# A hybrid decoder layer on one Trainium2 core: the hand-written order at the start of the FFN, carried on to the end of pair 1

## The chip, the cores and the metric

The kernel runs on one core of a Trainium2 chip. TensorE multiplies matrices, VectorE and GpSimd do elementwise work, ScalarE does copies, casts and activation functions, and SyncE issues most of the DMAs. The metric is the device time of one execution in microseconds, median of several runs; lower is better. The profile names the engines PE, DVE, POOL, ACT and SP, in this order.

## The reference

One layer for a prompt of 512 tokens and a sample group of 64 tokens, 576 in all, width 1024. The stage that matters here is the output projection of the mixer with its norms, and the first half of the feed-forward network (FFN):

```python
x = x + rms_norm(jnp.einsum('btd,de->bte', merged, w_out), norm_post_mix)
h = rms_norm(x, norm_pre_ffn)
gate, up = jnp.split(jnp.einsum('btd,df->btf', h, w_ffn_in), 2, axis=-1)
x = x + rms_norm(jnp.einsum('btf,fd->btd', jax.nn.silu(gate) * up, w_ffn_out), norm_post_ffn)
```

`gate` and `up` are 2816 wide each, 22 tiles of 128 columns.

## The kernel before

**Numbers in two parts.** Each fp32 operand is split into a high part (a cast on ScalarE) and a low part (operand minus high, on VectorE), and a product is three matmuls: high by high, high by low, low by high. `split` (activations) and `wsplit` (weights) emit the cast and the subtraction.

**Pairs.** The FFN's first half goes in 22 pairs; pair m is gate tile m and up tile m. For each pair the program does seven products (Strassen's scheme in Winograd's form over the two halves of the contraction and of the tokens) instead of eight. A product is four contraction tiles by three terms, twelve matmuls of 288 columns (`prod`). Steps 0 and 1, the "leads", take the plain activations B1 and the gate weights as loaded. Steps 2 to 6 take sums of activation quadrants (TQ[0] to TQ[3] and B2) and sums of weight quadrants, each split into two parts after it was made. Steps 2, 4 and 6 add up in PSUM bank p, steps 3 and 5 in bank e; after steps 2 and 3 ScalarE copies the bank (`as_`, `eu`), after steps 4, 5 and 6 VectorE reads it.

**Activation sums.** Token tiles 1 to 4 hold 128 prompt tokens, tile 0 the sample tokens. When a tile has its two norms, TensorE transposes it (`turn`). For tiles 1, 2 and 0 `left` splits it and copies it to `hf`; the tiles 3, 4 and the right part of tile 0 are then summed with it by class `Sums` (s3, s4, s0): `two` makes t[0] = b12 - b11 and t[1] = b22 - t[0] on VectorE, `late` makes t[1] - b11 and b21 - t[1] in place on GpSimd, and `split(i)` splits sum i. TQ[1] (step 2) holds t[1], TQ[0] (step 3) t[0], TQ[2] (step 4) the new b11, B2 (step 5) b22, TQ[3] (step 6) the new b21.

**Weight sums.** `pair_sums` makes the four sums in place in the raw gate and up tiles (`wraw` or `ad`, and `wup`), one of them always on GpSimd, all of them there for pair 0 (`slow`). Tiles are reused in rings: two `wraw`, two `wup`, two of each split pair (`w2`, `w22`, `w`), seven scratch tiles `ev`, five PSUM tiles `bank` and three `mmps`. A load into a reused tile waits until its last reader is done: pair 4's gate tile is loaded into pair 0's, pair 5's into pair 1's.

**What sets the order.** A scheduler orders the instructions of each engine by its own planning. Between `order.__enter__()` and `order.__exit__()` the instructions of TensorE, ScalarE, VectorE and GpSimd stand as written; the scheduler may still put later ones in between. Before, this written part covers the norms of the five tiles, the leads of pairs 0 to 3 and all splits of the activation sums; what follows (`run`, steps 2 to 6 of pair 0 and all other pairs) is left to the scheduler. SP's loads are always placed by it.

Of the kernel before, what the change touches and what calls it, by code (L numbers as in the profile page):

```python
# [93 lines left out]
def _build(ctx, tc, I, O):  # L94
# [1059 lines left out]
    class Sums:  # L1154
# [3 lines left out]
        def two(self):  # L1158
            b11, b12, b21, b22 = self.b
            self.t = [ev(KH * self.n).rearrange("p (a b) -> p a b", b=self.n) for _ in range(2)]  # L1160
            tt(self.t[0], b12, b11, ALU.subtract)
            tt(self.t[1], b22, self.t[0], ALU.subtract)

        def late(self):
            b11, b12, b21, b22 = self.b
            G.tensor_tensor(out=b11, in0=self.t[1], in1=b11, op=ALU.subtract)
            G.tensor_tensor(out=b21, in0=b21, in1=self.t[1], op=ALU.subtract)
# [14 lines left out]
    class Tile_:  # L1182
# [79 lines left out]
    def pair_sums(rg, ru, slow=False):  # L1262
        def sub(out, a, b, op=ALU.subtract, g=slow):
            (G if g else V).tensor_tensor(out=out, in0=a, in1=b, op=op)  # L1264

        a22 = two(fw, "w22", [P, KH, P], 2)
        S.copy(out=a22[0], in_=ru[:, KH:])
        sub(a22[1], ru[:, KH:], a22[0])
        sub(ru[:, KH:], ru[:, :KH], ru[:, KH:], ALU.add)
        sub(ru[:, :KH], rg[:, :KH], ru[:, :KH], g=True)  # L1270
        sub(rg[:, :KH], ru[:, KH:], rg[:, :KH])
        sub(rg[:, KH:], rg[:, KH:], rg[:, :KH])
        return a22

    def half_split(raw):
        g = two(fw, "w2", [P, KT, P], 2)
# [87 lines left out]
    prs = {}  # L1364
# [14 lines left out]
    act(warm, warm, AF.Silu)  # L1379
# [18 lines left out]
    ps = tile_mm(0)  # L1398
    wo_half(0, 0, ps)
# [10 lines left out]
    firsts = [pair_first(rg[0])]  # L1410
# [8 lines left out]
    firsts.append(pair_first(rg[1]))  # L1419
# [15 lines left out]
    av = [fp.tile([P, T], F32, name=f"av{k}") if not 4 <= k < 16 else None for k in range(FT)]  # L1435
    fwc = ExitStack()
    fw = fwc.enter_context(pool("fw", 1, reuse_waits="tile"))
    for m in range(4):
        raw = rg[m] if m < 2 else raw_load(dbl[m - 2][:, :KT * P].rearrange("p (k m) -> p k m", m=P), m * P)
        prs[m] = Pair(m, raw)  # L1440
        if m < 2:
            prs[m].w = firsts[m]
    ru = raw_up(0)
# [4 lines left out]
    prs[0].lead()  # L1448
    T_[3].turn(mmt)
    t4.resid()  # L1450
    prs[1].lead()
    prs[0].lead_out()
    t4.stat2()
    prs[2].first()
    s3 = Sums(*T_[3].pv, slice(C_OF[3], C_OF[3] + P), P)
    s3.two()
# [171 lines left out]
```

## Time and profile before

| | us |
|---|---|
| median of three runs | 1244.08 |
| lowest and highest of them | 1239.37, 1244.59 |
| the profiled execution | 1235.15 |
| its span, first to last instruction | 1233.4 |
| TensorE, VectorE, ScalarE, GpSimd busy | 1143.2, 720.1, 571.5, 150.0 |
| first matmul of pair 0's lead | 805.77 |
| first matmul of pair 0's step 2 | 835.52 |
| first matmul of pair 2's step 2 | 860.91 |

The last three are moments in the profiled execution, counted from the span's start. The idle time in brackets behind a row is that of the row's engine just ahead of it, and the name behind the arrow is what ended it. "L125" and the like are lines of helpers, so products are told apart by their tiles: `w` with `b1h` is a lead, `w22` or `w2` with `mh` or `b2h` one of the steps 2 to 6, `ident` a transpose.

### The profile page before, as it was taken

To read this page: it belongs to the slowest core of one execution; us is meant where nothing else is said; L and a number is where in the kernel's file an instruction comes from. 1 tells how busy PE (TensorE), PEld (TensorE's weight loads), DVE (VectorE), ACT (ScalarE), POOL (GpSimd) and SP (SyncE) were. 2 spreads that over 40 slices of the span, in tenths; PEclk is the share of its full clock that TensorE was granted. 3 is DMA by queue.
4 is the path that set the end of the run, shared out by engine and by line. 5 is a ranking of instruction groups with operands and counts; after the bars stand their busy time and mean duration, and the time that the engine had idled before them with its cause. 6 is when DMAs were issued, how large, how long until landed. Compare 5 with 4: busy or idle time off the path is not lost.

```text
span 1233.4 us, 20309 instructions
## 1 busy us (share of the span) xinstructions
PE 1143.2 (93%) x8104; PEld 1070.4 (87%) x8104; DVE 720.1 (58%) x1385; ACT 571.5 (46%) x1226; POOL 150.0 (12%) x227
## 2 busy tenths in 40 slices
PE   5699999999998998799998997978999999999997
PEld 4699999998997988698988895868999999978885
DVE  5136742566884456687554654677777888661323
ACT  4232532785554673377454533435454454441221
POOL 3200121001000011010000100141111110160001
PEclk9899999999997999899999999988999999999999
DMA  7730344333534353635133754022323332312222
GB/s 187 186 80 1 95 121 129 78 75 107 117 91 104 82 108 86 181 83 152 53 107 76 257 174 137 1 69 69 97 77 101 103 104 87 102 52 86 84 87 77
DMA packets 162001, 125.24 MB, mean 102 GB/s; under 512 B 13856, under 2 KB 144449, under 8 KB 161907
## 3 DMA queue, kind: packets, MB, share of 16 engines
q1 hardware_dynamic: 154770, 102.15, 31.4%
q0 software_dynamic: 6848, 21.22, 5.1%
q8 instruction: 63, 1.03, 0.3%
q10 hardware_dynamic: 288, 0.59, 0.2%
q14 instruction: 32, 0.25, 0.1%
HBM read 106.87 MB, written 17.06 MB: 100 GB/s over the span
## 4 chain that ended last, share of the span: by engine, by line
PE 43%; DMA 9%; issue 7%; DVE 5%; ACT 4%; POOL 1%; POOLq 0%; DVEq 0%; ACTq 0%; SPq 0%
PE mmps L267 11%; PE bank L1286 8%; PE bank L1561 6%; PE mmps L1561 6%; PE mmps L1286 5%; DMA wraw<-w_ffn_in 2%; PE bank L1179 2%; DMA out_sd_s<-Si 1%; PE mmps L1179 1%; DMA Si<-state_delta 1%; ACT whi L251 1%; DMA ev<-gcd 1%; DMA wraw<-w_out 1%; DVE wlo L125 1%; DVE w2lo L125 1%
## 5 line engine op out<-in xcount | busy, mean ns | idle before, releaser
L267 PE MATMUL mmps<-xh,whi 128*128 128x256 f32 (+1 forms) x896 | 274.2, 306 | 3.7 <-ACT ev L137 3.2
L267 PE MATMUL mmps<-xh,wlo 128*128 128x256 f32 (+1 forms) x896 | 271.4, 304 | 1.6 <-DVE wlo L125 1.6
L267 PE MATMUL mmps<-xl,whi 128*128 128x256 f32 (+1 forms) x896 | 272.5, 304 | 0.0
L125 DVE TENSOR_TENSOR wlo<-wraw,whi 128x1024 fp32r<-128x1024 f32 x114 | 147.4, 1293 | 211.5 <-ACT whi L251 211.3
L251 ACT CAST whi<-wraw 128x1024 fp32r<-128x1024 f32 x114 | 119.4, 1049 | 228.6 <-PE mmps L267 81.9
L267 PEld LDWEIGHTS mmps<-xh,whi 128*128 128x128 f32 x896 | 174.9, 195 | 6.7 <-ACT ev L137 4.2
L267 PEld LDWEIGHTS mmps<-xh,wlo 128*128 128x128 f32 x896 | 175.0, 196 | 2.3 <-DVE wlo L125 1.9
L267 PEld LDWEIGHTS mmps<-xl,whi 128*128 128x128 f32 x896 | 175.2, 196 | 0.4 <-issue 0.2
L128 DVE SCALAR_TENSOR_TENSOR ev<-ev,fcol 128x600 f32<-128x600 f32 x72 | 60.1, 837 | 1.8 <-ACT ev L137 0.6
L137 ACT ACT_TABLE_LOAD x41 | 52.6, 1283 | 6.9 <-DVE ans L125 2.6
L1286 PE MATMUL bank<-mh,w2hi 128*128 128x288 f32 x156 | 48.0, 308 | 4.8 <-ACT w2hi L251 4.7
L1286 PE MATMUL bank<-mh,w2lo 128*128 128x288 f32 x156 | 47.5, 305 | 2.3 <-DVE w2lo L125 2.3
L1286 PE MATMUL bank<-ml,w2hi 128*128 128x288 f32 x156 | 47.3, 303 | 0.0
L1264 POOL TENSOR_TENSOR wup<-wraw,wup 128x512 f32<-128x512 f32 x20 | 26.1, 1307 | 173.4 <-DVE wup L1264 173.3
L137 ACT ACTIVATE ev<-mmps 128x320 f32<-128x320 f32 (+1 forms) x73 | 30.7, 430 | 31.1 <-PE mmps L267 19.5
L137 ACT ACTIVATE jk<-bank 128x128 bf16<-128x128 f32 (+1 forms) x112 | 31.2, 279 | 25.3 <-PE bank L933 19.3
L378 PE MATMUL bank<-vh,xh 128*128 128x346 f32 (+1 forms) x96 | 31.1, 330 | 9.7 <-ACT vh L251 9.7
L267 PE MATMUL mmps<-oal,whi 128*128 128x320 f32 (+1 forms) x128 | 37.6, 296 | 1.0 <-DVE oal L125 1.0
L267 PE MATMUL mmps<-obl,whi 128*128 128x320 f32 (+1 forms) x128 | 37.9, 298 | 0.0
L267 PE MATMUL mmps<-oah,wlo 128*128 128x320 f32 (+1 forms) x128 | 37.5, 296 | 0.2 <-DVE wlo L125 0.2
L267 PE MATMUL mmps<-obh,wlo 128*128 128x320 f32 (+1 forms) x128 | 37.5, 296 | 0.0
L267 PE MATMUL mmps<-oah,whi 128*128 128x320 f32 (+1 forms) x128 | 37.2, 298 | 0.3 <-ACT oah L295 0.2
(500 smaller groups left out, 2989.0 us busy)
## 6 DMA issues: line engine op xcount, KB each, us to landing
wraw<-w_in SPq DMA_DIRECT2D x56, 512.0 KB, 8.6
wup<-w_ffn_in SPq DMA_DIRECT2D x22, 512.0 KB, 4.7
wraw<-w_ffn_out SPq DMA_DIRECT2D x22, 512.0 KB, 3.8
wraw<-w_ffn_in SPq DMA_DIRECT2D x20, 512.0 KB, 3.9
pgd<-ev POOLq DMA_DIRECT2D x16, 288.0 KB, 4.2
ev<-pgd SPq DMA_DIRECT2D x16, 288.0 KB, 8.3
wraw<-w_proj_b SPq DMA_DIRECT2D x8, 512.0 KB, 3.9
Si<-state_delta SPq DMA_DIRECT2D x8, 512.0 KB, 8.0
```

The lines of the kernel that those rows point to most:

```text
L125: V.tensor_tensor(out=out, in0=a, in1=b, op=op)
L128: V.scalar_tensor_tensor(out=out, in0=a, scalar=s, in1=b, op0=op0, op1=op1)
L137: return S.activation(out=out, in_=a, func=f, scale=scale, accum_out=accum)
L251: S.copy(out=hi, in_=raw)
L267: TE.matmul(ps, lhsT=a[:, j, :], rhs=b[k][:, HF[hf]], start=(k == 0 and i == 0), stop=(k == nk - 1 and i == 2))
L378: TE.matmul(ps, lhsT=a[k] if t == 0 else a[k][:, o:o + P], rhs=b[:, k, :c1 - c0], start=(k == 0 and q == 0), stop=(k == KT - 1 and q == le ...
L1179: TE.matmul(ps[q], lhsT=a[k] if t == 0 else a[k][:, o:o + P], rhs=b[k][:, q * 512:(q + 1) * 512], start=(k == 0 and i == 0), stop=(k == KT ...
L1264: (G if g else V).tensor_tensor(out=out, in0=a, in1=b, op=op)
L1286: TE.matmul(ps, lhsT=w[x][:, j], rhs=b[y][:, j], start=(first and j == 0 and i == 0), stop=(j == KH - 1 and i == 2), skip_group_check=not ...
L1561: TE.matmul(ps, lhsT=x[k] if t == 0 else x[k][:, o:o + P], rhs=unit[w][:, a_], start=(k == 0 and i == 0), stop=(k == FT - 1 and i == len(t ...
```

## The change

The written order goes on: it now also holds steps 2 to 6 of pairs 0 and 1 and the weight preparation of pairs 1 and 2, and the scheduler's part begins with `run(2)`. Within it:

- The chain of tile 4's second norm (`resid`, `stat2`, `scale`) comes ahead of the sums and of the Silu of the leads; `lead_out` is parted into the addition (`lead_add`) and the Silu (`lead_act`), and the Silus stand behind step 2 and later.
- The activation sums are made one at a time by `Sums.one(i)`, all on VectorE, each just ahead of its split and of the step that needs it; `two` and `late` are gone.
- The weight sums are all on VectorE; the first goes to a scratch tile `ev` (`s1`) instead of into `wup`, and the order of the quadrants is arranged anew, so that steps 3 and 6 take other split tiles (`w22` is now step 3, `w2` step 6; pair 0's step 2 has a `w22` tile of its own).
- Pair 0's bank e is an `mmps` tile, tile 4's transposes go to one `bank` and one `mmps`, and ScalarE's copy of pair 2's first bank stands ahead of the split of tile 3's b22 (`s3.split(4)`).
- `Pair.rest`, used for all later pairs, follows the new arrangement: one temporary more, nothing on GpSimd.

- The Silu on the one-column tile `warm` is written a few lines later; ScalarE's order around it is the same.

The matmuls are the same in number and shape. The diff, cut:

```diff
-        def two(self):
+        def one(self, i):
             b11, b12, b21, b22 = self.b
-            tt(self.t[0], b12, b11, ALU.subtract)
-            tt(self.t[1], b22, self.t[0], ALU.subtract)
-        def late(self):
-            G.tensor_tensor(out=b11, in0=self.t[1], in1=b11, op=ALU.subtract)
-            G.tensor_tensor(out=b21, in0=b21, in1=self.t[1], op=ALU.subtract)
...
+            out, x, y = ((self.t[0], b12, b11), (self.t[1], b22, self.t[0]), (b11, self.t[1], b11), (b21, b21, self.t[1]))[i]
+            tt(out, x, y, ALU.subtract)
...
-    def pair_sums(rg, ru, slow=False):
...
+        def sums(self):
+            ru, rg = raw_up(self.m) if self.m else ru0, self.rg
+            self.s1 = ev(KH * P).rearrange("p (k m) -> p k m", m=P)
+            tt(self.s1, ru[:, :KH], ru[:, KH:], ALU.add)
+            tt(ru[:, :KH], rg[:, :KH], ru[:, :KH], ALU.subtract)
+            tt(rg[:, :KH], self.s1, rg[:, :KH], ALU.subtract)
+            self.ru = ru
+        def sum4(self):
+            tt(self.rg[:, KH:], self.rg[:, KH:], self.rg[:, :KH], ALU.subtract)
...
     t4.scale()
-    a22 = pair_sums(rg[0], ru, True)
-    prs[1].lead_out()
-    s3.split(4)
...
+    p2_.p, p3_.p = bank()[:, :TH], bank()[:, :TH]
+    p2_.q = mmt()[:, :TH]
+    prod(p2_.p, p2_.w[0], BQ[0], True)
+    S.copy(out=p2_.g[:, L_], in_=p2_.p)
+    t4.turn(iter((bank, mmt)))
+    prod(p2_.q, p2_.w[1], BQ[1], True)
...
+    s3.split(4)
+    p1_.lead_add()
+    p3_.first()
+    s4.one(0)
+    s4.one(1)
...
+    p0_.sums()
+    p0_.w[2] = split_of("w22", p0_.rg[:, :KH], KH)
+    p0_.lead_act()
+    p1_.lead_act()
+    p0_.step(2)
+    p3_.lead_add()
     for x in (s0, s3, s4):
         x.split(0)
+    p0_.split1()
+    p0_.step(3)
+    p2_.lead_act()
+    p3_.lead_act()
+    for x in (s0, s3, s4):
+        x.one(2)
+        x.split(2)
+    p0_.split3()
+    p0_.step(4)
+    s0.split(4)
+    s4.split(4)
+    p0_.sum4()
+    p0_.w[5] = [g[:, KH:] for g in split_of("w2", p0_.rg, KT)]
+    p0_.step(5)
+    for x in (s0, s3, s4):
+        x.one(3)
+        x.split(3)
+    p1_.sums()
+    p1_.sum4()
+    p0_.step(6)
...
-    for m in range(FT):
+    for m in range(2, FT):
         run(m)
```

ScalarE between pair 0's steps 3 and 4. Before, the casts of the sums (`hf`) stand one behind the other, and the bank copies (`COPY ev`) come after them:

```order
L251 CAST w2hi<-wup 128x1024
L295 CAST mh<-hf 128x4x128
L295 CAST mh<-hf 128x4x32
L295 CAST mh<-hf 128x4x128
L295 CAST b2h<-hf 128x4x32
L295 CAST b2h<-mmps 128x4x128
L295 CAST mh<-hf 128x4x128
L295 CAST mh<-hf 128x4x32
L295 CAST mh<-hf 128x4x128
L251 CAST whi<-wraw 128x1024
L1346 COPY ev<-bank 128x288
L1351 COPY ev<-bank 128x288
```

Now, with step 3's copy (`COPY ev<-mmps`) first and pair 4's gate cast (`whi<-wraw`) behind step 5's weights:

```order
L1371 COPY ev<-mmps 128x288
L137 ACTIVATE av_8422<-av_8422 128x288
L137 ACTIVATE av_8423<-av_8423 128x288
L295 CAST mh<-hf 128x4x32
L295 CAST mh<-hf 128x4x128 x2
L251 CAST w2hi<-wup 128x1024
L295 CAST b2h<-hf 128x4x32
L295 CAST b2h<-mmps 128x4x128
L251 CAST w2hi<-wraw 128x1024
L1301 CAST whi<-wraw 128x1024
```

The copy and the two Silus moved ahead of the casts, and the up weights' cast (`w2hi<-wup`) behind them.

VectorE at the same place. Before, the low parts (`ml`, `b2l`) stand without sums between them:

```order
L125 TENSOR_TENSOR w2lo<-wup,w2hi 128x1024
L125 TENSOR_TENSOR ml<-hf,mh 128x4x128
L125 TENSOR_TENSOR ml<-hf,mh 128x4x32
L125 TENSOR_TENSOR ml<-hf,mh 128x4x128
L125 TENSOR_TENSOR b2l<-hf,b2h 128x4x32
L125 TENSOR_TENSOR b2l<-mmps,b2h 128x4x128
```

Now (`hf<-ev,hf` is a sum, `wraw<-wraw` the fourth weight sum, `ev<-bank,ev` the reading of step 4's bank):

```order
L125 TENSOR_TENSOR hf<-ev,hf 128x4x32
L125 TENSOR_TENSOR ml<-hf,mh 128x4x32
L125 TENSOR_TENSOR hf<-ev,hf 128x4x128
L125 TENSOR_TENSOR ml<-hf,mh 128x4x128
L125 TENSOR_TENSOR hf<-ev,hf 128x4x128
L125 TENSOR_TENSOR ml<-hf,mh 128x4x128
L125 TENSOR_TENSOR w2lo<-wup,w2hi 128x1024
L125 TENSOR_TENSOR ev<-bank,ev 128x288
L125 TENSOR_TENSOR b2l<-hf,b2h 128x4x32
L125 TENSOR_TENSOR b2l<-mmps,b2h 128x4x128
L125 TENSOR_TENSOR wraw<-wraw 128x512
L125 TENSOR_TENSOR w2lo<-wraw,w2hi 128x1024
```

Each sum now stands between two low parts, and the fourth weight sum behind the reading of step 4's bank.

VectorE a few rows on, at pair 0's step 6 (`wlo<-wraw,whi` is the low part of pair 4's gate tile, `av_8420<-mmps,ev` the reading of step 5's bank):

```order
L125 TENSOR_TENSOR av_8420<-mmps,ev 128x288
L125 TENSOR_TENSOR hf<-hf,ev 128x4x32
L125 TENSOR_TENSOR wlo<-wraw,whi 128x1024
L125 TENSOR_TENSOR ml<-hf,mh 128x4x32
L125 TENSOR_TENSOR hf<-hf,ev 128x4x128
L125 TENSOR_TENSOR ml<-hf,mh 128x4x128
L125 TENSOR_TENSOR hf<-hf,ev 128x4x128
L125 TENSOR_TENSOR ml<-hf,mh 128x4x128
L125 TENSOR_TENSOR ev<-wup 128x512
```

Here the scheduler put pair 4's low part between the last sums, and pair 1's first weight sum (`ev<-wup`) comes behind them; on TensorE pair 4's two leads stand between steps 5 and 6 of pair 0, 24 matmuls, as they did before in part. On GpSimd the written part of before held six weight sums and six activation sums, and each later pair one; now the norms' powers and, in the second half of the FFN, copies are all that is left there.

## Rows read from the trace of the kernel before

**Rows 1.** The page, part 1: busy us (share of the span) and instructions.

```profile
PE 1143.2 (93%) x8104; PEld 1070.4 (87%) x8104; DVE 720.1 (58%) x1385; ACT 571.5 (46%) x1226; POOL 150.0 (12%) x227
```

**Rows 2.** Stages: us, busy us by engine (instructions), clock, DMA share, GB/s.

```profile
805.77:835.50 29.73, 18.72 (x113) 16.96 (x111) 20.31 (x27) 11.61 (x21) 17.30 (x14) 0.88 0.25 66
835.50:850.20 14.70, 13.02 (x64) 11.62 (x65) 12.09 (x19) 9.77 (x19) 0.66 (x1) 0.66 0.25 72
850.20:860.90 10.70, 10.70 (x82) 10.70 (x81) 8.67 (x13) 5.38 (x10) 1.29 (x1) 1.00 0.33 98
...
950.00:1000.00 50.00, 50.00 (x379) 50.00 (x378) 40.57 (x54) 24.79 (x41) 5.95 (x5) 1.00 0.32 92
1000.00:1050.00 50.00, 50.00 (x378) 50.00 (x378) 40.44 (x56) 25.89 (x42) 6.13 (x5) 1.00 0.36 105
```

**Rows 3.** TensorE in order of time: start, us, instruction, [idle before <-releaser].

```profile
814.76 0.40 PE L1286 MATMUL bank<-b1h,whi 128*128 128x288 f32 x1 [1.60 <-ACT whi L251]
...
830.73 0.29 PE L1286 MATMUL mmps<-b1h,wlo 128*128 128x288 f32 x1
...
835.52 0.61 PE L1286 MATMUL bank<-mh,w2hi 128*128 128x288 f32 x1 [4.49 <-ACT w2hi L251]
...
837.70 0.44 PE L1286 MATMUL bank<-mh,w2hi 128*128 128x288 f32 x1
837.94 0.44 PE L1286 MATMUL bank<-ml,w2hi 128*128 128x288 f32 x1
...
850.25 0.29 PE L1286 MATMUL bank<-mh,w22hi 128*128 128x288 f32 x1
...
851.86 0.30 PE L1286 MATMUL bank<-mh,w2hi 128*128 128x288 f32 x1
...
860.91 0.30 PE L1286 MATMUL bank<-mh,w2hi 128*128 128x288 f32 x1
```

**Rows 4.** VectorE in order of time.

```profile
800.20 1.41 DVE L128 SCALAR_TENSOR_TENSOR x<-ev,x 128x512 f32<-128x512 f32 x2
...
818.19 2.82 DVE L128 SCALAR_TENSOR_TENSOR ev<-x,ev,np__7985 128x512 f32<-128x512 f32 x2
...
837.16 0.45 DVE L125 TENSOR_TENSOR av<-mmps,av 128x288 f32<-128x288 f32 x1
838.30 0.29 DVE L125 TENSOR_TENSOR ml<-ev,mh 128x128 fp32r<-128x128 f32 x1 [0.70 <-ACT mh L295]
838.82 1.29 DVE L125 TENSOR_TENSOR ml<-ev,mh 128x512 fp32r<-128x512 f32 x2 [0.23 <-ACT mh L295]
840.29 1.23 DVE L125 TENSOR_TENSOR w2lo<-wup,w2hi 128x1024 fp32r<-128x1024 f32 x1 [0.17 <-ACT w2hi L251]
```

**Rows 5.** ScalarE in order of time.

```profile
812.03 1.28 ACT L137 ACT_TABLE_LOAD   x1
813.33 0.44 ACT L137 ACTIVATE av<-av 128x288 f32<-128x288 f32 x1
...
830.84 0.62 ACT L295 CAST mh<-ev 128x512 fp32r<-128x512 f32 x1 [6.74 <-DVE ev L125]
...
834.42 1.05 ACT L251 CAST w2hi<-wraw 128x1024 fp32r<-128x1024 f32 x1
...
841.41 0.29 ACT L295 CAST b2h<-hf 128x128 fp32r<-128x128 f32 x1
841.61 0.57 ACT L295 CAST b2h<-mmps 128x512 fp32r<-128x512 f32 x1
...
844.27 0.39 ACT L1346 COPY ev<-bank 128x288 f32<-128x288 f32 x1
```

**Rows 6.** GpSimd in order of time.

```profile
818.87 1.60 POOL L1264 TENSOR_TENSOR wup<-wraw,wup 128x512 f32<-128x512 f32 x1
...
826.23 1.73 POOL L1166 TENSOR_TENSOR hf<-ev,hf 128x512 f32<-128x512 f32 x1
```

**Rows 7.** DMA issues, 800 to 860 us: count, KB each, median us to landing.

```profile
wraw<-w_ffn_in SPq DMA_DIRECT2D x2, 512.0 KB, 3.9
```

More of the change, by code (lines that the diff above doesn't have):

```diff
@@ L1260, in pair_first, with split_of @@
         return [[g[:, :KH] for g in g1], [g[:, KH:] for g in g1]]
-    def pair_sums(rg, ru, slow=False):
[L1263 to L1276, printed above, removed]
+    def split_of(nm, raw, n):
+        g = two(fw, nm, [P, n, P], 2)
         wsplit(raw, *g)
@@ L1378, in _build @@
     rg = [raw_gate(0), raw_gate(1)]
-    act(warm, warm, AF.Silu)
     ET = mybir.EngineType
@@ L1398, in _build @@
     ps = tile_mm(0)
+    act(warm, warm, AF.Silu)
     wo_half(0, 0, ps)
@@ L1409, in _build @@
     T_[0].stat2()
-    firsts = [pair_first(rg[0])]
+    prs[0] = Pair(0, rg[0])
+    prs[0].first()
     T_[0].scale()
@@ L1418, in _build @@
     norm2(2)
-    firsts.append(pair_first(rg[1]))
+    prs[1] = Pair(1, rg[1])
+    prs[1].first()
     wo_half(3, 1, ps)
@@ L1434, in _build @@
     dbl = [fp.tile([P, 2 * T], F32, name=f"ad{i}", tag=f"ad{i}") for i in range(2)]
-    av = [fp.tile([P, T], F32, name=f"av{k}") if not 4 <= k < 16 else None for k in range(FT)]
+    av += [fp.tile([P, T], F32, name=f"av{k}") if not 4 <= k < 16 else None for k in range(FT)]
     fwc = ExitStack()
     fw = fwc.enter_context(pool("fw", 1, reuse_waits="tile"))
[L1438 to L1443, printed above, removed]
+    for m in (0, 1):
+        prs[m].g = av[m]
+    for m in (2, 3):
+        prs[m] = Pair(m, raw_load(dbl[m - 2][:, :KT * P].rearrange("p (k m) -> p k m", m=P), m * P))
+    ru0 = raw_up(0)
+    p0_, p1_, p2_, p3_ = (prs[m] for m in range(4))
     t4 = T_[4]
@@ L1447, in _build @@
     t4.stat1()
-    prs[0].lead()
+    p0_.lead()
     T_[3].turn(mmt)
+    s3 = Sums(*T_[3].pv, slice(C_OF[3], C_OF[3] + P), P)
+    p2_.first_hi()
     t4.resid()
-    prs[1].lead()
-    prs[0].lead_out()
+    p0_.lead_add()
+    p1_.lead()
+    s3.one(0)
+    p2_.first_lo()
     t4.stat2()
-    prs[2].first()
-    s3 = Sums(*T_[3].pv, slice(C_OF[3], C_OF[3] + P), P)
-    s3.two()
+    s3.one(1)
     t4.scale()
-    a22 = pair_sums(rg[0], ru, True)
-    prs[1].lead_out()
-    s3.split(4)
-    p, q = prs[2].banks("p"), prs[2].banks("q")
@@ new lines, in _build @@
+    p0_.step(3)
[17 more added lines that the diff above has]
+    p0_.step(6)
+    p1_.split2()
+    p1_.split1()
+    p1_.split3()
+    p1_.step(2)
+    p1_.step(3)
+    p2_.sums()
@@ L1490, in _build @@
+    p2_.sum4()
+    p1_.step(4)
+    p1_.step(5)
+    p2_.split2()
+    p1_.step(6)
+    p2_.split1()
+    p2_.split3()
     order.__exit__(None, None, None)
```

83 lines of the change are left out of this document (44 added, 39 removed).

## The prediction

> **What bounds the kernel now.** I read the page first: TensorE is busy for 93% of the span and no other engine is near that [rows 1]. An average over stages says little about one of them, so the second view was the table of stages. From 850.20 on TensorE is full at the full clock (10.70 of 10.70 us, later twice 50.00 of 50.00): nothing that happens to VectorE there can give time back. The gap lies before: from 805.77 to 835.50 only 18.72 of 29.73 us are busy, and from 835.50 to 850.20 the granted clock is 0.66 [rows 2]. The third view, the instructions in order of time, shows what the gap is made of. A product of twelve matmuls takes 1.61 us at the full clock (850.25 to 851.86); in the slow stretch the spacing is 0.24 us instead of 0.13 (837.70 to 837.94). TensorE waits 1.60 us for a cast at 814.76, ends its eight first ("lead") products at 831.0, and waits 4.49 us at 835.52 for the weights of pair 0's step 2 [rows 3]. In 805.77 to 860.91 there is work for some 34 us (20 products of 1.61 and 16 transposes), and 55 us pass. The change rewrites just this stretch, so its worth is the moment at which pair 2's first product starts: 860.91 before. Both orders put the same 20 products (eight leads, two of pair 4, ten of pairs 0 and 1) and 16 transposes ahead of it, and after it TensorE is full, so what is late or early there stays so to the end.
>
> **Prices.** VectorE: 0.69 us for 128x512 and 0.29 for 128x128, 0.45 for 128x288, 1.23 for 128x1024, and back to back each starts 0.09 before its forerunner ends (two of 0.69 in 1.29) [rows 4]. ScalarE: 1.05 for a cast of 1024, 0.57 of 512, 0.29 of 128, 0.39 for a copy of 288, 0.44 for a Silu, with the same overlap [rows 5]. A hand-over between engines costs 0.04 (the cast at 834.42 ends at 835.47, TensorE starts at 835.52) [rows 3, 5]. A weight load takes 3.9 us from issue to landing [rows 7]. With these I walked the new order engine by engine from 805.77, where both programs are still alike.
>
> **Part one, the leads and the norm chain: a gain.** Today the two scalings of token tile 4 take 2.82 us, because GpSimd's sums run beside them; the same pair alone takes 1.41 [rows 4, 6]. In the new order nothing runs on GpSimd there, pair 0's sums come later, and the Silu with its table load is moved behind the leads. VectorE then has pair 2's low weights at 811.7 and the scaled rows at 813.9, and TensorE runs through to 814.7. One wait stays: ScalarE copies pair 2's first bank (ends 815.1) before it casts the part of tile 3 that frees the PSUM bank (815.6), VectorE subtracts (816.4), and only then the second four transposes start: 1.45 us lost. Forty instructions follow without a gap, so the leads end at 821.8, 9.2 us before the 831.0 of today. Behind them VectorE must still do tile 4's and tile 0's first sums, their low parts and three weight sums in a row; the third ends at 823.6, its cast at 824.3. Pair 0's step 2 starts at 824.3 instead of 835.5: **11.2 us early**.
>
> **Part two, pair 0's five steps: a larger loss.** Today they and pair 4's two leads run from 835.52 to 852.0, in 16.5 us, because all sums were made before: GpSimd did six activation sums (1.73 us for a wide one), and the casts and low parts then follow each other in threes [rows 3, 6]. In the new order each sum stands in VectorE's queue directly ahead of its own split, and ScalarE's queue holds a copy that waits for TensorE. Step 2 ends at 826.5 and step 3, after a copy, three casts and a weight cast, runs from 829.0 to 831.1. Then ScalarE copies step 3's bank (831.5) and does two Silus (832.2) before it casts tile 0's b11 (832.4). VectorE, which has stood since 829.8, subtracts (832.75), makes tile 3's sum (833.35), waits for its cast (834.0), subtracts (834.7), makes tile 4's sum (835.3), waits again (835.9); behind that cast comes the cast of the up weights (836.9). Step 4 starts at 836.9: a wait of 6.0 us. It ends at 839.7; only then VectorE adds (840.1), does two low parts and the fourth weight sum (841.5), ScalarE casts (842.6) and step 5 starts: 3.2 us more. With its low part (843.9) gate buffer 0 is free and SP issues pair 4's load, which in both orders uses that buffer: landed 847.8, cast 849.0. In TensorE's order pair 4's 24 matmuls stand ahead of step 6, and in VectorE's order pair 4's low weights stand ahead of the last activation sums, so both queues stop behind that load: 3.7 us for TensorE. Step 6 runs from 854.4 to 856.1. Pair 0 takes 31.8 us where it took 16.5: 15.3 lost against 11.2 won, **4.1 late**.
>
> **Part three, pair 1.** Its four sums follow on VectorE (857.2), the cast ends at 858.2 and step 2 starts there after a wait of 2.2. Steps 2 and 3 end at 862.6. Step 4 needs step 2's bank copied, and the copy stands behind pair 5's weight cast, which waits for a load issued when pair 1's low weights are done (859.4 + 3.9 + 1.05 = 864.4): it starts at 864.8, a wait of 2.4. Step 6 waits 0.5 for an addition that stands behind four sums of pair 2. Pair 2's first product starts at 870.4 instead of 860.9: **9.5 late**. Its second one waits 1.4 us for a bank that VectorE frees late, where the old order lost 0.5 us in all in this pair: **10.4**.
>
> **The clock.** This is the one term that no row of the old order gives. Today the slow spacing reigns in the stretch with clock 0.66 [rows 2, 3], after a wait of 4.49 us, and the waits of the new order are as long. Unharmed the sum is 10.4; with the slow spacing from 829 to 855 steps 3 and 4 are each 1.1 longer on this chain (step 5 hides behind the load): 12.4. I take 12, nearer to the slow end, since the row at 835.52 shows TensorE slow after such a wait.
>
> **Table load.** It moves from ahead of pair 2's cast to ahead of step 2's copy, where ScalarE waits for TensorE anyway: 1.28 us by the row, and the Silu behind it starts at once [rows 5]; the two Silus end at 826.2, the copy can start at 826.5. So it is free. The Trainium skill's page "ScalarE: Activation LUTs" (What ACT_TABLE_LOAD costs) puts a drain of about 1.38 us behind each load; here the row shows 0.02 us, and by the page's figure the copy would start 1.1 us later and the sum would be 1.1 higher.
>
> **Later pairs.** From pair 2 on each pair has one sum more on VectorE (four of 0.69 instead of three, the fourth was GpSimd's). VectorE is busy 40.57 of 50 us, thus 9.1 of a pair's 11.3; 9.7 still fits [rows 2]. I cost it at nothing; the cover is TensorE's own backlog.
>
> **Rivals.**
> 1. Forecast: the queues stop each other as walked. +10.4 to +12.4, with 2 us more or less for hand-overs and loads: +8 to +15.
> 2. The early start is kept (faster). It needs pair 0's steps to take the old 16.5 us although sums and splits alternate, which would be so if casts and sums overlapped across tiles. Then 11.2 us are won: -11. It decides from a pair 0 of under 26 us on. Against it: VectorE already stands for ScalarE's casts (0.70 at 838.30), ScalarE 6.74 us for VectorE's sum at 830.84; neither overtakes [rows 4, 5].
> 3. Within the noise: both loads come in time, because the buffer waits that I put ahead of them end early (3.7 and 2.4 us back): +4 to +6.
> 4. VectorE becomes the bound: the added sum shows in each of the 18 pairs behind pair 3 that before had it on GpSimd, 18 x 0.69 = 12.4 on top: +24. Half of it, or a slow clock up to 870 us (2.2 more), gives +15 to +20. For it: VectorE's share is already 81%; against it, TensorE does not wait once in the two stretches of 50 us [rows 2].
>
> **How the numbers follow.** The profiled execution took 1235.15 us (span 1233.4 and 1.75 around it); +12 makes 1247. It is 8.9 us below the median of the three runs, 1244.08, and a difference in one stage carries over, so I predict 1244.08 + 12 = 1256. Chances: forecast 0.64, rival 2 0.11, rival 3 0.14, rival 4 0.11. A measurement of this kernel tells some 0.5% (6.2 us) from no change. Faster by more: rival 2, 0.11. Within: rival 3, 0.14. Slower: the others, 0.75. The range leaves out rival 2 and the upper half of rival 4: from +0 to +20, thus 1244 to 1264.
>
> **What would show it.** Right: the last lead product ends near 822, step 2 of pair 0 starts near 824, TensorE waits 5 to 7 us for a cast of the up weights near 837, then 3 to 4 us for a cast behind a load, pair 2 starts near 871, and from 885 on TensorE is full and GpSimd empty. Wrong: pair 0's five steps in less than 26 us (then rivals 2 or 3), or idle TensorE in 900 to 1050 (then rival 4). What would break the walk is an engine that takes its queue in another order than the program's, or loads that land much sooner than 3.9 us.

## The result and the profile after

| | before | after |
|---|---|---|
| median (us) | 1241.72 of 4 runs | 1275.58 of 4 runs |
| lowest and highest | 1237.29, 1244.59 | 1271.05, 1278.99 |
| the profiled execution | 1235.15 | 1278.89 |

The change makes the kernel slower by 2.8%: the ratio is 1.0284, with a 95% interval of 1.0250 to 1.0317. In a second comparison on another occasion it was 1266.41 against 1237.00, ratio 1.0240 (1.0204 to 1.0276). The forecast was 1256 with a range to 1264: the direction held, the size did not, +29 to +34 us instead of +12.

The page of after, part 1, answers [rows 1]:

```profile
PE 1160.5 (91%) x8104; PEld 1081.4 (85%) x8104; DVE 722.3 (57%) x1418; ACT 570.5 (45%) x1227; POOL 107.4 (8%) x195
```

Its stages, with the columns of [rows 2]:

```profile
831.00:847.00 16.00, 7.11 (x26) 5.63 (x26) 6.97 (x13) 8.80 (x18) 0.00 (x0) 0.63 0.00 0
847.00:861.00 14.00, 8.10 (x28) 6.56 (x28) 5.83 (x11) 2.63 (x5) 0.00 (x0) 0.50 0.25 75
...
900.00:950.00 50.00, 46.61 (x344) 45.69 (x344) 36.69 (x56) 22.12 (x37) 0.00 (x0) 1.00 0.30 85
950.00:1000.00 50.00, 47.48 (x352) 46.67 (x351) 36.01 (x54) 22.16 (x39) 0.00 (x0) 1.00 0.29 85
```

TensorE is no longer full behind 900 (46.61 and 47.48 of 50 us; the kernel before had 50.00 from 950 on), and VectorE is not what it waits for by load: it is busy for 36.69 of 50, less than the 40.57 of before. Between 831 and 861 the granted clock is at 0.63 and 0.50 (0.50 is the lower of its two levels, 1.2 of 2.4 GHz).

TensorE in order of time, the first matmul of each product that waits; these rows answer [rows 3]:

```profile
831.50 0.40 PE L1271 MATMUL bank<-mh,w22hi 128*128 128x288 f32 x1 [3.43 <-ACT w22hi L251]
...
837.24 0.40 PE L1271 MATMUL mmps<-mh,w22hi 128*128 128x288 f32 x1 [2.24 <-ACT w22hi L251]
...
846.37 0.61 PE L1271 MATMUL bank<-mh,w2hi 128*128 128x288 f32 x1 [5.85 <-ACT w2hi L251]
...
853.42 0.61 PE L1271 MATMUL mmps<-b2h,w2hi 128*128 128x288 f32 x1 [3.02 <-ACT w2hi L251]
...
859.50 0.61 PE L1271 MATMUL mmps<-b1h,whi 128*128 128x288 f32 x1 [2.05 <-ACT whi L1301]
...
876.34 0.61 PE L1271 MATMUL bank<-mh,w2hi 128*128 128x288 f32 x1 [2.20 <-ACT ev L1366]
...
883.21 0.40 PE L1271 MATMUL bank<-mh,w2hi 128*128 128x288 f32 x1 [0.37 <-ACT w2hi L251]
```

In this execution the first lead starts at 812.30, 6.53 us later than the 805.77 of before, although both programs are the same up to there; over all traces of this study that moment lies between 801.7 and 813.1. So I count from the first lead. Pair 2 starts 70.91 us behind it (883.21), 55.14 in before: 15.8 late. The last matmul of the FFN's first half starts at 1121.17, 308.9 behind the first lead; in before 1077.47, thus 271.7. Of the 43.7 us between the two profiled executions 6.5 lie ahead of the change, 15.8 between the first lead and pair 2, and 21.4 in pairs 2 to 21. Nothing is left for the second half.

### The profile page after: what moved, and what is told of

It reads as the page before. It is cut to its first block, busy times and chain, and to the rows that moved or that the text cites. A ratio compares the mean times of both kernels' runs of the same rounds, so it can differ in the third digit from the quotient of the medians.

```text
span 1277.1 us, 20221 instructions
## 1 busy us (share of the span) xinstructions
PE 1160.5 (91%) x8104; PEld 1081.4 (85%) x8104; DVE 722.3 (57%) x1418; ACT 570.5 (45%) x1227; POOL 107.4 (8%) x195
## 4 chain that ended last, share of the span: by engine, by line
PE 38%; DMA 12%; DVE 7%; issue 6%; ACT 6%; POOL 0%; POOLq 0%; DVEq 0%; ACTq 0%; SPq 0%
PE mmps L267 10%; PE bank L1271 6%; PE bank L1617 6%; PE mmps L1617 5%; DMA wraw<-w_ffn_in 5%; PE mmps L1271 2%; DVE w2lo L125 2%; PE bank L1177 2%; ACT w2hi L251 2%; PE mmps L1177 1%; DMA out_sd_s<-Si 1%; ACT whi L1301 1%; DMA Si<-state_delta 1%; DMA wraw<-w_out 1%; DMA ev<-gcd 1%
## 5 line engine op out<-in xcount | busy, mean ns | idle before, releaser
L125 DVE TENSOR_TENSOR wlo<-wraw,whi 128x1024 fp32r<-128x1024 f32 x114 | 139.3, 1222 | 223.5 <-ACT whi L251 197.7
L251 ACT CAST whi<-wraw 128x1024 fp32r<-128x1024 f32 x94 | 98.7, 1051 | 204.9 <-PE mmps L267 75.8
L1271 PEld LDWEIGHTS bank<-mh,w2hi 128*128 128x128 f32 x152 | 30.7, 202 | 13.8 <-ACT w2hi L251 10.0
L378 PE MATMUL bank<-vh,xh 128*128 128x346 f32 (+1 forms) x96 | 31.6, 336 | 10.4 <-ACT vh L251 10.4
```

What stands on the lines that cost most here:

```text
L125: V.tensor_tensor(out=out, in0=a, in1=b, op=op)
L251: S.copy(out=hi, in_=raw)
L378: TE.matmul(ps, lhsT=a[k] if t == 0 else a[k][:, o:o + P], rhs=b[:, k, :c1 - c0], start=(k == 0 and q == 0), stop=(k == KT - 1 and q == le ...
L1271: TE.matmul(ps, lhsT=w[x][:, j], rhs=b[y][:, j], start=(first and j == 0 and i == 0), stop=(j == KH - 1 and i == 2), skip_group_check=not ...
```

## Where the later pairs lose: a ring through the gate load

The chain of waits of after, in order of time (start, us, what; short links are left out), shows two pairs of the steady part:

```profile
951.33 3.79 DMA wraw<-w_ffn_in
...
955.14 1.06 ACT whi L1301
...
956.23 1.22 DVE wlo L125
957.45 0.60 DVE ev L125
958.05 0.37 DVE avxb L125
...
958.94 0.45 DVE ev L125
959.39 0.60 DVE w22lo L125
959.99 0.60 DVE wraw L125
960.59 0.38 DVE avxb L125
...
961.65 1.06 ACT w2hi L251
...
962.73 1.23 DVE w2lo L125
...
963.99 3.87 DMA wraw<-w_ffn_in
...
967.87 1.05 ACT whi L1301
...
968.97 4.00 PE bank L1271 x28
```

The gate load (`wraw`, 3.8 us) starts when the low part of gate sums (`w2lo`, 962.73) has read a gate tile for the last time. It is followed by the cast (955.14) and the low part (956.23) of the new gate tile, and then, in VectorE's queue, by the four weight sums of the pair ahead of it (one in the scratch tile `ev`, one in `wup`, two in `wraw`), three bank readings (`avxb`, `ev`, `avxb`) and `w22lo`; only then comes the cast of these sums (961.65), their low part, and the next load. One round took 12.66 us (951.33 to 963.99) and the next 11.40 (to 975.39); in the second TensorE is drawn in: its lead waits 1.28 us for the gate cast and starts at 968.97, and the next cast of sums waits for it. Sixteen gate casts on end are 12.0 us apart on the mean, and a pair's seven products take TensorE 7 x 1.61 = 11.27; in before sixteen casts are 11.0 apart. Sixteen rounds of 1.0 us more make 16 to 17 of the 21.4 us; 2.8 more belong to the last pair of this execution, from the last gate cast to the last product (13.8 us, in the second profile of the changed kernel 11.1), with the clock at 0.90 in 1100 to 1150. TensorE's own waits between pair 2 and the last product point the same way: they add up to 15.7 us, 11.2 of them for the gate cast, against 1.5 us in before, 0.5 of them for the gate cast. There are two gate buffers, and the Trainium skill's page "Trainium Kernel Development and Optimization" (Best Practices) advises double-buffering so that DMA and compute overlap. Here the trace shows both buffers in use, and TensorE works during the loads; what does not overlap are the sums in one buffer and the load of the other, because VectorE's order puts the low part that waits for the load ahead of the sums.

The same ring was in the kernel before, and this is VectorE there:

```profile
950.64 1.24 DVE L125 TENSOR_TENSOR wlo<-wraw,whi 128x1024 fp32r<-128x1024 f32 x1 [1.27 <-ACT whi L251]
951.80 0.68 DVE L1264 TENSOR_TENSOR wraw<-wup,wraw 128x512 f32<-128x512 f32 x1
952.52 0.69 DVE L1264 TENSOR_TENSOR wraw<-wraw 128x512 f32<-128x512 f32 x1
...
955.02 1.23 DVE L125 TENSOR_TENSOR w2lo<-wraw,w2hi 128x1024 fp32r<-128x1024 f32 x1 [0.82 <-ACT w2hi L251]
```

Behind the low part (950.64) stand just two sums in the gate tile; their cast starts at 953.96, `w2lo` follows, and the next gate load is issued at 956.28. From gate cast to gate cast (949.55 to 960.06) it takes 10.5 us in this round: 0.8 less than TensorE's pair, and TensorE is full. That is the reserve that the change used up.

**The two halves alone.** Old weight sums from pair 3 on, in the changed kernel, and new ones in the kernel before:

```diff
 # e1_old_rest, class Pair of the changed kernel
         def rest(self):
+            if self.m > 2:
+                return self.old_rest()   # sums of the kernel before
# e2_new_rest, class Pair of the kernel before
-            a22 = pair_sums(self.rg, ru, slow)
...
+            s1 = ev(KH * P).rearrange("p (k m) -> p k m", m=P)
+            tt(s1, ru[:, :KH], ru[:, KH:], ALU.add)
+            tt(ru[:, :KH], rg[:, :KH], ru[:, :KH], ALU.subtract)
+            tt(rg[:, :KH], s1, rg[:, :KH], ALU.subtract)
+            tt(rg[:, KH:], rg[:, KH:], rg[:, :KH], ALU.subtract)
```

> The changed kernel with its whole written order, but from pair 3 on the weight sums are made as before: one of the four on GpSimd, the up tile's own sum in place, the old use of the split tiles. Two theories of the 21 us that pairs 2 to 21 lose. Load loop: the gate load, its cast, its low part, the sums in the gate tile, their cast and low part and the next load follow each other in a ring; the new sums make that ring longer than a pair's 11.26 us on TensorE. Then this kernel is 15 to 20 us faster than the changed one (1256 to 1261 us), TensorE has 49.5 us or more of 50 from 900 on, and only the 16 us of the start are left over the kernel before. Late start: the loads come late because the written part ends late, and never catch up. Then the old sums change little: within 5 us of the changed kernel, and the waits for the gate weights' cast stay.

> The kernel before with nothing changed but the weight sums of pairs 1 to 21: all four on VectorE, one in a temporary, the new use of the split tiles; the start keeps its old order. Load loop: the loss of the later pairs shows here without the new start, 12 to 21 us over the kernel before (1254 to 1263 us), with waits of TensorE for the gate weights' cast in 900 to 1050. Late start: within 4 us of the kernel before.

e1_old_rest took 1252.44 against 1237.49, ratio 1.0121 (1.0092 to 1.0150); e2_new_rest 1251.97, ratio 1.0119 (1.0088 to 1.0151). So the start costs 15 us and the later pairs 14.5, each without the other, and their sum is the 29.4 us of the second comparison (e1_old_rest is 14 us under the changed kernel there, a little less than the 15 to 20 expected). In 900 to 1050 TensorE does not wait once in e1_old_rest; in e2_new_rest it waits seven times, 7.7 us, each time for the gate cast. A late start is not what slows the later pairs. The first stage of e2_new_rest from 900 on:

```profile
900.00:950.00 50.00, 47.53 (x355) 47.01 (x354) 36.02 (x54) 22.82 (x39) 0.00 (x0) 1.00 0.29 85
```

**More buffers.**

```diff
+        if m in (6, 7, 10, 11):
+            raw = fp.tile([P, 2 * T], F32, name=f"adw{m}", tag=f"ad{m % 2}")
+            return raw_load(raw[:, :KT * P].rearrange("p (k m) -> p k m", m=P), m * P)
...
-    for k in (4, 8, 12, 14):
+    for k in (4, 8):
```

(The output tiles that share these two buffers are handed out later, in pairs 10 and 11.)

> The changed kernel with the gate tiles of pairs 6, 7, 10 and 11 loaded into the two tiles that held those of pairs 2 and 3, so that pairs 4 to 11 have four gate buffers and the pairs behind them two as before. VectorE does the same work. Load loop: with four buffers a load no longer waits for the low part of the pair just ahead, TensorE is full up to about pair 11 (some 985 us) and waits only behind it; 5 to 10 us faster than the changed kernel (1266 to 1271 us). VectorE's own work as the bound (rival 4 as the prediction put it): no difference between the pairs with four buffers and those with two, within 3 us of the changed kernel.

It took 1267.63, ratio 1.0243 (1.0210 to 1.0277): no faster than the changed kernel's 1.0240, so the time missed what was expected (the 1266 to 1271 us were counted from the first median, 1275.58; beside the 1266.41 of the second comparison nothing is won). The trace shows half of it. TensorE's waits in 885 to 985, first of the changed kernel (first profile), then of e3_four (total, times, longest):

```profile
PE bank L1271 <- ACT whi L1301: 4.1, 3, 1.6
```

```profile
PE mmps L1274 <- ACT ev L1369: 2.0, 4, 0.5
PE bank L1274 <- ACT ev L1369: 0.5, 1, 0.5
```

(Of the first only the line on the gate cast is shown; in the second profile of the changed kernel it is 5.0 us in four waits.) With four buffers the waits for the gate cast are gone, and TensorE has 48.48 and 49.02 of 50 us where the second profile of the changed kernel has 47.39 and 46.96: 3.2 us of the 5.7 that were lost. Waits for ScalarE's bank copies, 0.5 us each, come up instead and keep the rest, and pair 2 started 1.0 us later here (69.86 behind the first lead against 68.84). By this run the ring causes the waits for the gate cast, but not all of the loss.

**The written order ended early.** This was meant for the start:

```diff
+    order.__exit__(None, None, None)
     p0_.sums()
...
     p2_.split1()
     p2_.split3()
-    order.__exit__(None, None, None)
```

> The changed kernel with the written order ended behind the leads: the same instructions follow in the program, but the scheduler orders pair 0's and pair 1's steps, their sums and splits. If the written order of sums and splits is what makes the start late (each sum ahead of its own split, the copies and Silus between), the wait ahead of step 4 falls under 3 us and pair 2 starts 4 to 9 us earlier than in the changed kernel; the later pairs lose as much as they do there: 1267 to 1272 us. If the start is late because all sums were put on VectorE and made late, whoever orders them, pair 2 starts within 3 us of the changed kernel's and the time is within 4 us of it.

It took 1249.81, ratio 1.0111 (1.0073 to 1.0149), some 17 us better than the changed kernel where 4 to 9 were expected. TensorE is busy for 14.30 of 15.00 us in 835 to 850 here. All sums are on VectorE as in the changed kernel, so neither their engine nor their number made the start late: it was the order written for this part, on all four engines together. What is left over the kernel before is the loss of the later pairs, whose gate casts are again some 11.2 and 12.8 us apart by turns. So this kernel served as the base for three more runs.

**Which part of the new sums.** e8_old_on_vector keeps the old arrangement but has its GpSimd sum on VectorE; e9_new_on_gpsimd keeps the new one and has its gate-minus-up sum on GpSimd; e10_low_behind changes no instruction, only that the low part of the next gate tile must follow the last weight sum of the pair ahead, as it does in the program's text:

```diff
 # e8_old_on_vector, in old_rest
-            G.tensor_tensor(out=ru[:, :KH], in0=rg[:, :KH], in1=ru[:, :KH], op=ALU.subtract)
+            tt(ru[:, :KH], rg[:, :KH], ru[:, :KH], ALU.subtract)
 # e9_new_on_gpsimd, in sums
-            tt(ru[:, :KH], rg[:, :KH], ru[:, :KH], ALU.subtract)
+            (G if self.m > 2 else V).tensor_tensor(out=ru[:, :KH], in0=rg[:, :KH], in1=ru[:, :KH], op=ALU.subtract)
 # e10_low_behind, in begin
-            prs[m].first()
+            prs[m].first_hi()
+            with tc.issue_after(prs[m - 1].last.ins):   # the fourth weight sum
+                prs[m].first_lo()
```

> e5_ends_old with one thing changed: the one weight sum of pairs 3 to 21 that is on GpSimd there goes to VectorE; the old arrangement of the sums stays. Ring of the loads: this sum reads the gate tile and now stands in VectorE's queue, where the low part of the next pair's gate tile may hold it up; the ring grows by one sum, 0.6 us, from 10.7 to 11.3, about a pair's 11.26 on TensorE: 0 to 4 us slower than e5_ends_old (1234 to 1238 us), gate casts 11.2 to 11.5 us apart. Rival (the sum on VectorE alone makes the later pairs slow, whatever the arrangement): 10 to 15 us slower than e5_ends_old, as e4_ends was.

> e4_ends with one thing changed: of the new weight sums of pairs 3 to 21 the one that makes gate minus up goes to GpSimd; the new arrangement with the sum in a temporary stays. Ring of the loads: one sum leaves VectorE's queue behind the low part, but the first sum, the two in the gate tile, the low part of the temporary and two bank readings still follow it; the ring falls from 12.0 to 11.4 to 11.7 us, 4 to 8 us faster than e4_ends (1242 to 1246 us). Rival (the sum on VectorE alone is the cause): all of the loss goes, 1234 to 1237 us.

> e4_ends with one thing changed: in every later pair the low part of the next pair's gate tile must stand behind the last weight sum of the pair before it in VectorE's queue, which is their order in the program, while the scheduler puts it ahead. All four sums stay on VectorE, in the new arrangement. Ring of the loads (load 3.9, cast 1.05, low part 1.2, sums 2.9 to 4.1, cast 1.05, low part 1.2, then the next load): the sums no longer wait for the load, the ring is opened, the gate casts come 11.2 to 11.3 us apart, TensorE has 49.5 of 50 us or more in 900 to 1050, and nearly all of e4_ends's 12 us come back: 1236 to 1241 us. Rival (VectorE has too much to do, or the new arrangement needs its split tiles too early): within 3 us of e4_ends, gate casts still 12.0 us apart on the mean.

| | median (us) | ratio to before | gate casts apart (us) |
|---|---|---|---|
| e4_ends: new sums, all on VectorE | 1249.81 | 1.0111 (1.0073 to 1.0149) | 12.0 |
| e9: new sums, one on GpSimd | 1251.45 | 1.0136 (1.0102 to 1.0170) | 12.0 |
| e10: as e4, low part behind the sums | 1240.16 | 1.0031 (1.0007 to 1.0055) | 11.4 |
| e5: old sums, one on GpSimd | 1234.17 | 0.9970 (0.9946 to 0.9994) | 11.0 |
| e8: old sums, all on VectorE | 1235.21 | 1.0007 (0.9984 to 1.0030) | 11.0 |

The spacing is the mean over sixteen pairs. Stages of e8, e9 and e10:

```profile
900.00:950.00 50.00, 49.90 (x374) 49.56 (x374) 38.86 (x59) 24.57 (x39) 0.00 (x0) 1.00 0.29 85
```

```profile
950.00:1000.00 50.00, 46.89 (x347) 46.05 (x346) 33.74 (x50) 21.57 (x36) 5.13 (x4) 1.00 0.29 85
```

```profile
900.00:950.00 50.00, 50.00 (x379) 50.00 (x378) 37.42 (x58) 25.87 (x43) 0.00 (x0) 1.00 0.36 105
...
1000.00:1050.00 50.00, 48.66 (x367) 48.43 (x366) 37.20 (x57) 23.32 (x38) 0.00 (x0) 1.00 0.33 96
```

The fourth sum on VectorE costs 3 to 5 us at most by the medians and the ratios of e5 and e8, whose intervals overlap, and nothing in the trace, where TensorE stays full. Taking one sum off VectorE gives nothing back in the new arrangement (e9, where I had expected 4 to 8 us). The rows of the kernel before show why the engine of this sum matters so little:

```profile
960.52 1.29 POOL L1264 TENSOR_TENSOR wup<-wraw,wup 128x512 f32<-128x512 f32 x1 [9.72 <-DVE wup L1264]
...
961.14 1.75 DVE L125 TENSOR_TENSOR wlo<-wraw,whi 128x1024 fp32r<-128x1024 f32 x1 [0.76 <-ACT whi L251]
```

Beside GpSimd's sum VectorE's low part took 1.75 us; in the ten rounds from 950 to 1050 it took 1.24 to 2.16 and ended 1.08 to 1.09 us behind GpSimd's sum each time, where it takes 1.23 in e8 without a sum on GpSimd. In e9 `w22lo` took 1.09 to 1.29 us beside that sum instead of 0.69. So a sum on GpSimd takes some 0.6 us out of VectorE's queue and, where the two meet, puts up to 0.9 us back into the instruction beside it. What costs is the order: with the same instructions, e10 has VectorE like this,

```profile
950.50 0.68 DVE L125 TENSOR_TENSOR wraw<-ev,wraw 128x512 f32<-128x512 f32 x1
...
951.47 0.68 DVE L1317 TENSOR_TENSOR wraw<-wraw 128x512 f32<-128x512 f32 x1
952.07 1.22 DVE L125 TENSOR_TENSOR wlo<-wraw,whi 128x1024 fp32r<-128x1024 f32 x1
...
953.57 1.22 DVE L125 TENSOR_TENSOR w2lo<-wraw,w2hi 128x1024 fp32r<-128x1024 f32 x1
```

both sums of the gate tile ahead of the low part `wlo`, and the loss over the kernel before falls from 12.3 to 5.0 us (by the ratios, from 13.7 to 3.8). TensorE is full in 900 to 950 and lacks 0.7 to 1.3 us of 50 behind it. Its only waits there are again for the gate cast, 0.67 us at 971.82 and 1.34 us at 1006.95, and each stands behind a gate load that took longer than the 3.6 to 3.7 us of others in this trace: 4.70 us from 966.00 on, and

```profile
1000.44 5.39 DMA wraw<-w_ffn_in
```

Why these two loads took longer, no run here shows. The bad order is the scheduler's: with the old sums it had the split of the up tile's half and the up tile's own sum ahead of the low part, with the new ones the temporary's split, and by turns its sum too, come behind it.

## Where the start loses: turns between two engines, and the clock

The start cost 13.7 to 15.8 us at pair 2 in the traces of the changed kernel, where I had walked 9.5. ScalarE (first) and VectorE of after, between steps 2 and 4, show the turns that the prediction named:

```profile
831.47 1.28 ACT L137 ACT_TABLE_LOAD   x1
832.76 0.78 ACT L137 ACTIVATE av<-av 128x288 f32<-128x288 f32 x2
...
842.77 0.62 ACT L295 CAST mh<-hf 128x512 fp32r<-128x512 f32 x1 [0.96 <-DVE hf L125]
...
845.28 1.04 ACT L251 CAST w2hi<-wup 128x1024 fp32r<-128x1024 f32 x1
```

```profile
841.85 0.29 DVE L125 TENSOR_TENSOR ml<-hf,mh 128x128 fp32r<-128x128 f32 x1 [3.57 <-ACT mh L295]
842.06 0.68 DVE L125 TENSOR_TENSOR hf<-ev,hf 128x512 f32<-128x512 f32 x1
843.43 0.69 DVE L125 TENSOR_TENSOR ml<-hf,mh 128x512 fp32r<-128x512 f32 x1 [0.69 <-ACT mh L295]
844.04 0.68 DVE L125 TENSOR_TENSOR hf<-ev,hf 128x512 f32<-128x512 f32 x1
```

Sum, cast, low part, sum (842.06, 842.77, 843.43, 844.04): VectorE stands 0.69 us for a cast, ScalarE 0.96 for a sum. The up weights' cast ends at 846.32, and step 4 starts at 846.37.

```diff
 # e6_sums_first
     p0_.w[2] = split_of("w22", p0_.rg[:, :KH], KH)
+    for x in (s0, s3, s4):
+        x.one(2)
+    for x in (s0, s3, s4):
+        x.one(3)
...
     p0_.split1()
+    p0_.sum4()
     p0_.step(3)
...
-        x.one(2)
         x.split(2)
...
-    p0_.sum4()
...
-        x.one(3)
         x.split(3)
# e7_fill: fill(n) puts n matmuls into the bank of pair 1's step 3
+    fill(22)
     p0_.step(2)
...
+    fill(14)
     p0_.step(3)
...
+    fill(36)
     p0_.step(4)
...
+    fill(18)
     p0_.step(5)
```

> The changed kernel unchanged, beside the next three on the same chip: 28 to 34 us over the kernel before (some 1266 to 1272 us where the kernel before takes 1237.5).

> The changed kernel with its six in-place activation sums (the third and fourth of each tile) put directly behind the low part of step 2's weights, and pair 0's fourth weight sum ahead of step 3, so that no sum stands between two splits any more; the same instructions otherwise. Theory (sum, cast, low part by turns on two engines, and the fourth sum behind the reading of step 4's bank): the wait ahead of step 4 falls from 5.9 to 3.5 us, the one of 3.0 ahead of step 5 is gone, pair 4's gate load starts 4 to 6 us earlier and with it pair 2: 4 to 8 us faster than the changed kernel. Rival (the copies, Silus and casts on ScalarE alone set the pace, and the sums hide behind them): within 2 us of it.

> The changed kernel with 90 more matmuls on TensorE (22, 14, 36 and 18 of 128x288 ahead of steps 2, 3, 4 and 5 of pair 0, into the bank of pair 1's step 3, which starts afresh later), so that TensorE works through its four waits there: about 11.9 us of work at the full clock where 14.5 us are waited. Theory of the clock (the waits lower the granted clock, and the slow spacing of 0.24 us is what stretches each of the steps 2 to 4 by 1.2 us and pair 4's leads and step 6 further): the granted clock of that stretch stays over 0.9, a step takes about 2.1 us instead of 3.5, pair 2 starts 4 to 6 us earlier, 3 to 6 us faster than the changed kernel in spite of the added work. Rival (a step is stretched by its operands, which come in parts): the steps keep their 3.3 to 4.1 us, and the time is the same or up to 4 us longer.

after_again took 1266.41. e6_sums_first took 1258.38, ratio 1.0172 (1.0135 to 1.0209): 8 us faster with seven sums in another place, the six activation sums and pair 0's fourth weight sum; what each of the two moves is worth was not tried. TensorE there, steps 4 and 5 of pair 0:

```profile
837.33 0.61 PE L1271 MATMUL bank<-mh,w2hi 128*128 128x288 f32 x1 [3.46 <-ACT w2hi L251]
...
842.71 0.40 PE L1271 MATMUL mmps<-b2l,w2hi 128*128 128x288 f32 x1 [1.11 <-DVE b2l L125]
```

The wait ahead of step 4 is 3.46 us instead of 5.85, the one ahead of step 5 is gone (what is left in it, 1.11 us, is for a low part), and pair 2 starts 59.6 us behind the first lead, 9 to 11 us earlier than in the two traces of the changed kernel.

e7_fill took 1268.62, ratio 1.0257 (1.0227 to 1.0286), not faster. Its stage and TensorE's rows (the fills are those of `b1h,whi`):

```profile
835.00:850.00 15.00, 11.50 (x79) 10.34 (x77) 7.50 (x12) 5.17 (x10) 0.00 (x0) 1.00 0.17 50
```

```profile
830.17 2.02 PE L1511 MATMUL bank<-b1h,whi 128*128 128x288 f32 x14
832.57 0.40 PE L1271 MATMUL mmps<-mh,w22hi 128*128 128x288 f32 x1 [0.38 <-ACT w22hi L251]
...
834.90 4.96 PE L1511 MATMUL bank<-b1h,whi 128*128 128x288 f32 x36
```

The clock is at 1.00 where it was 0.50 to 0.63, and step 3 starts at 832.57 and the next fill behind it at 834.90, 2.33 us later; in after the copy that follows step 3 came 3.3 us behind its start (837.24, 840.55). Pair 2 starts 64.3 us behind the first lead, 4.5 us earlier than in after_again. So the clock does stretch the steps. The Trainium skill's page "TensorE: Matmul & The Clock Gate" (HAM oscillation — how this bites in real kernels) describes the same of a kernel that waits between bursts of matmuls: the clock falls in the wait, and the next burst starts slow. The traces agree, with 0.50 to 0.63 where TensorE waited and 1.00 where the fills ran. But the time did not fall. In the trace the ring of the later pairs and a slower last pair (clock 0.90 in 1100 to 1150 against 1.00 in after_again) had eaten the gain: 302.2 us to the last product against 301.9. So I took the ring away:

> e1_old_rest with the 90 added matmuls of e7_fill ahead of steps 2 to 5 of pair 0. In e7_fill the granted clock stayed at 1.00 in 835 to 850 and pair 2 started 4.5 us earlier, but the time did not fall. If that gain was eaten by the ring of the loads and the last pair behind it, which these old sums remove, the time is now 3 to 5 us under e1_old_rest's 1252.4: 1247 to 1250 us. If the fill itself costs what the clock gives (its last matmuls run into the steps), it is within 2 us of e1_old_rest.

e11_fill_old took 1253.26, ratio 1.0146 (1.0118 to 1.0173), where e1_old_rest without the fill had 1.0121: again not faster, though its trace has 283.8 us to the last product against 290.0. Both kernels once more, side by side:

> The kernel e1_old_rest once more (the new start, from pair 3 on the old weight sums), beside the next one on the same chip, to settle what the clock is worth: as before some 15 us over the kernel before, 1250 to 1253 us.

> The kernel e11_fill_old once more: e12_no_fill with the 90 added matmuls that keep the granted clock up through the waits of pair 0. In the traces the stretch from the first lead to the last product of the FFN's first half was 283.8 us with the added matmuls and 290.0 without, but the medians of the two were the same within their intervals. If the clock is worth what the traces say, this one is 3 to 6 us faster than e12_no_fill; if the traces showed one lucky execution each, they are within 1.5 us and the clock term of the loss is nearer to nothing.

1254.44 (ratio 1.0142, 1.0122 to 1.0162) without the fill, 1252.27 (1.0122, 1.0101 to 1.0142) with it: the intervals overlap. The traces have 288.9 and 283.1 us to the last product, but the one with the fill reached its first lead at 813.09, the other at 807.21, and both spans are 1252.0. In all three pairs of traces pair 2 starts earlier with the fill, by 4.5, 5.9 and 5.6 us; that the time gets it back is not shown, since what lies ahead of the first lead scatters as much. This stays open.

**Both repairs.**

> Both repairs in one: the written order ends behind the leads, as in e4_ends, and the weight sums from pair 3 on are those of the kernel before, as in e1_old_rest. If the two losses are independent (the start 16 us, the load loop of the later pairs 14 us) nothing of them is left: within 6 us of the kernel before, TensorE at 49.5 of 50 us or more from 900 on. Whether it is faster depends on the leads alone, which end 9 us earlier: pair 2 starts up to 5 us ahead of before's 860.9, counted from the same first lead, so 0 to -5 us. If instead the old sums need the old start (their loads and GpSimd's sums placed as they were), 5 us or more of the loss stay.

e5_ends_old took 1234.17, ratio 0.9970 (0.9946 to 0.9994): all of the loss is gone, and it is the one kernel whose interval lies below 1. Of the new leads' gain it keeps a part: step 2 of pair 0 starts 24.7 us behind the first lead, after a wait of 8.1 us for its weights, where before had it at 29.7 and the written order at 19.2; the last product comes 2.6 us earlier than in before (269.1 us behind the first lead). From 900 on TensorE is full:

```profile
900.00:950.00 50.00, 50.00 (x378) 50.00 (x377) 38.05 (x56) 25.94 (x42) 6.48 (x5) 1.00 0.36 106
```

## The prediction, step by step

- **Leads and norm chain: right.** Counted from the first lead I had their end at 16.0 us and step 2 at 18.5; they came at 15.8 and 19.2. The one wait among them was 0.92 us instead of 1.45, and the two scalings, with nothing on GpSimd beside them, took 1.41 us (at 819.02) as priced.
- **Pair 0's steps: right in kind, too short.** The waits ahead of steps 4 and 5 were forecast as 6.0 and 3.2 us and were 5.85 and 3.02; the load and pair 4's lead held TensorE for 2.05 us (forecast 3.7), pair 1's steps 2 and 4 waited 2.10 and 2.20 (2.2 and 2.4). What failed is the length of the steps themselves. One reading was off: of pair 4's 24 lead matmuls 8 run behind 852.0 in before (853.72 and from 855.18 on), so its 16.5 us hold 16 of them and not both leads; at 0.13 us each this moves 1.1 us from pair 0 to pair 1, and the 9.5 at pair 2 stays.
- **The clock term: mis-sized.** I priced the unharmed sum at 10.4 and slow steps 3 and 4 at 2.0 more. In after step 2 was slow too (831.50 to its copy at 835.03), and the clock was still at 0.50 in 847 to 861 and at 0.51 in 861 to 866, where I had let it rise at 855. With the clock held up by the fills pair 2 starts 9.2, 9.9 and 9.2 us later than in before, and the walk without any clock term had 9.5. So the queues were priced about right, and the term is 4.5 to 5.9 us at this place, not 2; it may be more, since the fills end ahead of 850 and the clock of e7_fill was at 0.69 in 850 to 861. By the medians the start alone cost 15 us (e1_old_rest) where the forecast had 12.
- **Table load: right.** The rows at 831.47 and 832.76 show the Silu 0.01 us behind the load, and ScalarE then waited for TensorE. The Trainium skill's page "ScalarE: Activation LUTs" (What ACT_TABLE_LOAD costs) adds a drain of about 1.38 us to each load. In these rows it shows neither behind the load nor ahead of it, where the cast before it ends 0.02 us earlier.
- **Later pairs "at nothing": wrong,** and this is the step that broke the forecast: put at 0, they cost 14.5 us (e2_new_rest). I compared VectorE's busy time with a pair's length (9.1 and 9.7 of 11.3), and saw no wait of TensorE in before. Both readings were true and neither was the question: the limit was a ring through load, casts, low parts and sums, 10.5 us long in a round of before against TensorE's 11.27, and 12.0 on the mean in after, and it could have been read from VectorE's and ScalarE's rows of one pair.
- **Rival 4** came nearest in time, +24, but as a mechanism it fell: VectorE was no bound, it was idle 13 us of 50, and e8 has the added sum at little or no cost. Rivals 2 and 3 fell with the start.

## What to carry to other kernels

An engine that is never waited for can still be part of a ring that is nearly as long as the loop: where a load waits for a buffer, add up load, casts and everything that stands between them in each queue, for one round, and compare that with the round of the engine that bounds. A change that only regroups instructions can move them to the wrong side of a queue entry that waits for a load; with a scheduler in between, look at the order that it makes. And where two engines hand work to each other, try all steps of one kind first (the sums, then the casts): here every change of turns cost both engines a wait (0.69 and 0.96 us), and the regrouping won 8 us.

## What I had not expected of the hardware

Ninety added matmuls in front of the waiting steps kept the granted clock at 1.00 in 835 to 850 (e7_fill), and pair 2 started 4.5 to 5.9 us earlier with more work done. And the part of the program ahead of the change, the same in all kernels, ends between 801.7 and 813.1 us after the span's start, with a clock of 0.88 to 0.93 between 500 and 600: a difference of 5 us in one pair of profiles says nothing unless it is counted from a common mark.
